# Two heads' values side by side in the array, and a Fourier half of whole 128 by 128 tiles

## The chip, the cores and the metric

The kernel runs on one core of a Trainium2 chip. The metric is the device time of one launch in microseconds (us); lower is better. The core has a matmul engine (TensorE, PE in the profile, with PEld for its weight loads), VectorE (DVE), ScalarE (ACT), GpSimd (POOL) and SyncE (SP), which here issues all DMAs. A matmul holds a stationary operand of up to 128 rows by 128 columns in the array and streams a moving operand of up to 512 columns past it; sums land in PSUM, one PSUM partition for each column of the array.

## The reference

Two layers of an encoder trunk over 512 positions and 1024 channels. Each layer splits its projection into a Fourier group of 512 channels, and 8 query heads, 2 key heads and 2 value heads of 64 channels.

```
h = rmsnorm(x); p = h @ w_in
u, q, k, v = split(p)
y_f = real(fft2(u, norm="ortho")) @ w_fourier + b_fourier
q, k = rope(rmsnorm(q)), rope(rmsnorm(k))
y_a = attention(q, k, v)      # blocks of 128 queries against a band of 384 keys, |i-j| <= 128, a sink logit per head
x = x + concat(rmsnorm(y_f), rmsnorm(y_a)) @ w_o
h = rmsnorm(x)
gate, val = split(dwconv3(h @ w_up))
x = x + (silu(gate) * val) @ w_down
```

## The kernel before

Everything is held transposed or in blocks of 128 positions, so that each matmul has 128 positions or channels on the partitions. In layer 0 the Fourier half and the product of probabilities and values use float32 operands; a float32 matmul shows as two records in the profile. In layer 1 (and in both layers for the large projections) each operand is split in a rounded part and a rest, both float32r, and `mm3` (lines 118 to 122) issues three matmuls of one record each: high by high, rest by high, high by rest. `put` and `split` make such pairs: ScalarE writes the high part, VectorE subtracts it to make the rest.

The Fourier half works on folded data. Since cosines are even and sines odd, 512 columns fold to 257 even ones (0 to 256) and 255 odd ones. They are cut in rows or columns of 128, 128 and 1 for the even part, and 128 and 127 for the odd part. Each of the three steps (the projection `pee`/`poo`, then two transform stages in lines 577 to 606, then the product with `w_fourier` in lines 615 to 643) thus has matmuls with 127 or 1 columns in the array, and the single last row 256 (`tail`, `ut`) meets a one-row table `alts` (tile `altr`) or the last row of W_fourier (`wtr`, `wt`) in matmuls with one row.

Attention goes by pairs of heads (`attention(p, ...)`, p in the order 3, 0, 1, 2). For each head e of the pair and each query block i: scores (line 506), scaling, mask and minimum on VectorE (510), exponential on ScalarE (513), normalising on GpSimd (515), transposition by TensorE (518) and a copy to `pT`. After the four blocks of a head come four matmuls (one for each key block j, line 527) that sum values into `py`. The values lie in `vz`, 64 zero columns on each side and in between, and a window of 128 columns of it is the stationary operand:

```
c0 = 128 * g + 64 * (1 - e)
lhs = [v[:, j, c0:c0 + P] for v in vp]
```

So the head's 64 columns land in the upper or lower half of `py`, and the zeros add nothing to the other half. In layer 1 there are two tiles vz and two pT, high part and rest.

The order on each engine is set by a scheduler that works from the program's dependences and its own cost table; the written order is only its input. It interleaves the Fourier half, attention, and the first half of the output projection (`proj`), whose matmuls are tied to the transpositions in `steps`. PSUM banks are drawn from four pools ("mm" 3, "sc" 2, "tp" 2, "av" 1), and temporary tiles from pools of fixed depth (`TEMPS`). While layer 0's feed-forward part runs, `presplit` loads and splits layer 1's weights and keeps them in DRAM.

Of the kernel before, what the change touches and what calls it, by code (L numbers as in the profile page):

```python
# [16 lines left out]
P = 128  # L17
# [7 lines left out]
NB = S // P  # L25
# [12 lines left out]
def encoder_kernel(tc, t):  # L38
# [34 lines left out]
    TEMPS = {"act": (1024, 8), "m4": (1024, 5), "slab": (1028, 4), "pT": (2560, 2),  # L73
# [75 lines left out]
    def presplit(l):  # L149
# [33 lines left out]
        for j in range(NF):  # L183
            jobs.append((lambda j=j: [wload(t["w_fold"][l, j], 1024, temp(1024, "m4"))], [f"f{j}"]))
# [90 lines left out]
    def zero_values(l):  # L275

        v = [cp.tile([P, NB, 320], F32R if l else F32, tag=f"vz{s}", name=nm("vz")) for s in range(1 + l)]
        for z in v:
            nc.gpsimd.memset(f(z) if l else z, 0.0)
        return v  # L280

    def load_tables(l):
        tab = []
        for i in range(2):
            if l:
                raw = temp(512, "m4")
                nc.sync.dma_start(raw, t["dft"][i])
                tab.append([cp.tile([P, 512], F32R, tag=f"t{z}{i}", name=nm("tab")) for z in "hl"])
                split(*tab[i], raw)
            else:  # L290
                tab.append([cp.tile([P, 512], F32, tag=f"th{i}", name=nm("tab"))])
                nc.sync.dma_start(tab[i][0], t["dft"][i])
        alt = cp.tile([1, 258], F32R if l else F32, tag="altr", name=nm("altr"))
        if l:
            raw = temp(258, "m4")[:1]
            nc.sync.dma_start(raw, t["alt"])
            act(alt, raw)
        else:
            nc.sync.dma_start(alt, t["alt"])
        return tab, alt  # L300

    vp = zero_values(0)
# [33 lines left out]

    def fold_wf(raw, w=None):
        w = temp(512, "tA") if w is None else w
        tt(w[:, :256], raw[:, :256], raw[:, 512:768], ALU.add)
        tt(w[:, 256:], raw[:, 256:512], raw[:, 768:], ALU.subtract)  # L340
        return w
# [11 lines left out]
    for l in range(L):  # L353

        r1 = col_rstd(acc, 1.0 / D)
        qraw = {}
        for grp in (1, 0):
# [16 lines left out]
            for b in range(NB):  # L374
                act(z[:, b, :n], pq[b][:, :n], scale=r1[:, b:b + 1])
                if grp:
                    o = [v[:, b, 64:320].rearrange("p (g d) -> p g d", g=2)[:, :, :64] for v in vp]
                    put(o, pq[b][:, 256:384].rearrange("p (g d) -> p g d", g=2), r1[:, b:b + 1])
# [103 lines left out]
        off = [0, 2, 5, 8]  # L482
# [3 lines left out]
        def attention(p, first_pair):  # L486
            g = p // 2
            py = psum("av")
            first = True
            if not l:  # L490
                both = temp(2560, "pT").rearrange("p (e b q) -> p e b q", e=2, q=P)
            for e in range(2):
                h = 2 * p + e
                nmax, den = [sp.tile([P, NB], F32, tag=z, name=nm(z), bufs=3) for z in ("nmax", "den")]
                if l:
                    pT = temp(2560, "pT", F32R).rearrange("p (s b q) -> p s b q", s=2, q=P)
                    pT = [pT[:, s] for s in range(2)]
                else:
                    pT = [both[:, e]]
                for i in range(NB):  # L500
                    j0, j1 = max(0, i - 1), min(NB - 1, i + 1)
                    n = (j1 - j0 + 1) * P
                    m0 = P if i == 0 else 0
                    sc = psum("sc")
                    for s in range(2):
                        nc.tensor.matmul(sc[:, :n], qT[p][:, e, i * P:(i + 1) * P], kT[g][:, s, j0 * P:(j1 + 1) * P],  # L506
                                         start=s == 0, stop=s == 1)
                    pr = temp(385, "tA")
                    nc.gpsimd.tensor_copy(pr[:, n:n + 1], nsink[:, l, h:h + 1])  # L509
                    nc.vector.tensor_tensor_reduce(  # L510
                        out=pr[:, :n], in0=sc[:, :n], in1=mask[:, m0:m0 + n], scale=qs_scale[p][:, i, e:e + 1],
                        scalar=nsink[:, l, h:h + 1], op0=ALU.add, op1=ALU.min, accum_out=nmax[:, i:i + 1])
                    act(pr[:, :n + 1], pr[:, :n + 1], AF.Exp, scale=-1.0, bias=nmax[:, i:i + 1], accum_out=den[:, i:i + 1])
                    nc.vector.reciprocal(den[:, i:i + 1], den[:, i:i + 1])
                    nc.gpsimd.tensor_scalar(pr[:, :n], pr[:, :n], den[:, i:i + 1], 1.0, op0=ALU.mult, op1=ALU.mult)
                    pp = psum("tp")
                    for j in range(n // P):
                        tr = nc.tensor.transpose(pp[:, j * P:(j + 1) * P], pr[:, j * P:(j + 1) * P], ident)  # L518
                    steps.append(tr.ins)
                    put([z[:, off[i]:off[i] + n // P, :].rearrange("p b q -> p (b q)") for z in pT], pp[:, :n])  # L520
                c0 = 128 * g + 64 * (1 - e)
                for j in range(NB):
                    i0, i1 = max(0, j - 1), min(NB - 1, j + 1)
                    st = off[i0] + j - max(0, i0 - 1)
                    rhs = [z[:, st:st + 2 * (i1 - i0) + 1:2, :] for z in pT]
# [8 lines left out]
        if l == 0:  # L534
            tabs, alts = load_tables(l)
# [23 lines left out]
        def tail_out(pe, scale):  # L559
            b = halves(tp.tile([1, 2, 258], F32R if l else F32, tag="tail", name=nm("tail"), bufs=2))[:1 + l]  # L560
            put(b, pe[2][:1, :258], scale)
            return b

        def stage_out(pe, po, scale):
            tiles = []
            if not l:
                two = temp(1028, "slab")
            for m in range(2):
                a = halves(pair("slab", 514)) if l else [two[:, m * 514:(m + 1) * 514]]
                n = P - m  # L570
                put([z[:, :258] for z in a], pe[m][:, :258], scale)
                put([z[:n, 258:514] for z in a], po[:n, m * 256:(m + 1) * 256], scale)
                tiles.append(a)
            return tiles, tail_out(pe, scale)

        ue, ut = stage_out(pee, poo, 1.0)
        for stage in range(2):
            pe = [psum(), psum(), psum("sc")]
            po = psum()
            for m, (c0, c1) in enumerate(((0, 128), (128, 256), (256, 257))):  # L580
                o = pe[m][:c1 - c0, :258]
                for i in range(2):
                    if stage == 0:
                        mm3(o, [z[:, c0:c1] for z in ue[i]], [z[:, 0:258] for z in tabs[i]], i == 0, False)
                    else:
                        mm3(o, [z[:, c0:c1] for z in tabs[i]], [z[:, 0:258] for z in ue[i]], i == 0, False)
                for z in ut:
                    if stage == 0:
                        nc.tensor.matmul(o, z[:, c0:c1], alts, start=False, stop=z is ut[-1])
                    else:  # L590
                        nc.tensor.matmul(o, alts[:, c0:c1], z, start=False, stop=z is ut[-1])
            for m in range(2):
                n = P - m
                o = po[:n, m * 256:(m + 1) * 256]
                for i in range(2):
                    kn = P - i
                    u2 = [z[:kn, 258:514] for z in ue[i]]
                    t2_ = [z[:kn] for z in tabs[i]]
                    st = m == 0 and i == 0
                    if stage == 0:  # L600
                        mm3(o, [z[:, 1 + m * P:1 + m * P + n] for z in u2], [z[:, 256:512] for z in t2_],
                            st, i == 1, skip_group_check=True)
                    else:
                        mm3(o, [z[:, 257 + m * P:257 + m * P + n] for z in t2_], u2,
                            st, i == 1, skip_group_check=True)
# [9 lines left out]
        for j in range(NF):  # L615
# [3 lines left out]
            wtr = sp.tile([1, P], F32, tag="wtr", name=nm("wtr"), bufs=1)  # L619
            nc.sync.dma_start(wtr, t["w_fourier"][l, 256:257, c0:c1])  # L620
            if l:
# [218 lines left out]
```

## Time and profile before

| | before |
|---|---|
| median of 3 runs | 1075.63 us (1074.64 to 1077.24) |
| the profiled execution | 1076.12 us |
| its span | 1074.3 us |
| TensorE busy / weight loads | 1060.8 us (99%) / 881.9 us (82%) |
| VectorE, ScalarE, GpSimd busy | 737.2, 510.4, 118.4 us |
| DMA | 142.13 MB, 132 GB/s over the span |

All times in the profile count from the span's start. The tiled stages of layer 0 that the change touches lie between about 60 and 158 us, those of layer 1 between about 550 and 680 us; the rest is projections and the feed-forward part. "Busy" of a TensorE record runs to its modelled end, which overlaps the next record's start: how fast matmuls follow one another is read from their starts. In a row of the timeline stand the start, the time to the end of the last record, the engine, the line, the operation, out<-in, the array's rows\*columns in use, the moving operand, and the count.

### The profile page before, as it was taken

The page shows a single profiled execution, that of the slowest core. Times are in us where ns is not written, and L with a number is a line of the kernel's source. Part 1 is how long each engine was busy: PE and PEld are TensorE (multiplying, and loading weights), DVE is VectorE, ACT ScalarE, POOL GpSimd, SP SyncE. Part 2 cuts the span into 40 slices and gives each one's busy share as a digit, 9 for nine tenths or more (in the row PEclk, how much of TensorE's full clock was granted, in tenths as well). Part 3 has the DMA queues.
Part 4 walks back from the last instruction along what each step waited for, and adds up shares of the span by engine and source line. Part 5 has one row for each costly group of instructions (what it writes and reads, how often), then busy time and mean ns, then how long its engine had stood idle before and what let it go on. Part 6 is the DMA issues. An engine that isn't in the chain of part 4 may idle for free.

```text
span 1074.3 us, 14345 instructions
## 1 busy us (share of the span) xinstructions
PE 1060.8 (99%) x5075; PEld 881.9 (82%) x5075; DVE 737.2 (69%) x1364; ACT 510.4 (48%) x940; POOL 118.4 (11%) x171
## 2 busy tenths in 40 slices
PE   8999999999999999999999999999999999999998
PEld 7866888888888888888899887888888888888887
DVE  7856767697767777776619788387887336777632
ACT  5338755454544445455414775155554224444421
POOL 1134410000000000000001442001211000101000
PEclk9999999999999999999999999999999999999999
DMA  7242162333259932338856322423332333233241
GB/s 276 83 138 84 36 196 79 99 98 98 86 174 372 367 99 97 99 104 297 299 182 212 112 70 79 138 79 99 98 99 81 101 106 100 85 102 94 81 147 47
DMA packets 58859, 142.13 MB, mean 132 GB/s; under 512 B 6554, under 2 KB 19108, under 8 KB 58788
## 3 DMA queue, kind: packets, MB, share of 16 engines
q1 hardware_dynamic: 58788, 141.22, 40.3%
q8 instruction: 40, 0.66, 0.3%
q14 instruction: 31, 0.25, 0.1%
HBM read 118.12 MB, written 23.07 MB: 131 GB/s over the span
## 4 chain that ended last, share of the span: by engine, by line
PE 92%; DVE 4%; ACT 1%; DMA 1%; issue 1%; SPq 0%; POOL 0%; DVEq 0%; ACTq 0%
PE ps L120 27%; PE ps L122 27%; PE ps L121 27%; PE ps L118 5%; PE ps L506 2%; PE ps L518 2%; DMA wraw<-in_w_qkv_dram 1%; DVE act L93 1%; PE ps L224 1%; DVE tF L96 1%; PE ps L217 1%; DVE tA L510 0%; PE ps L464 0%; DVE tF L93 0%; DVE slab L93 0%
## 5 line engine op out<-in xcount | busy, mean ns | idle before, releaser
L90 ACT ACTIVATE whi<-wraw 128x512 fp32r<-128x512 f32 (+1 forms) x296 | 181.9, 616 | 297.8 <-PE ps L122 281.4
L93 DVE TENSOR_TENSOR wlo<-wraw,whi 128x512 fp32r<-128x512 f32 (+1 forms) x304 | 221.9, 732 | 115.5 <-ACT whi L90 113.9
L120 PE MATMUL ps<-act,whi 128*128 128x512 f32 x768 | 298.9, 390 | 0.0
L121 PE MATMUL ps<-act,wlo 128*128 128x512 f32 x768 | 298.7, 389 | 0.0
L122 PE MATMUL ps<-act,whi 128*128 128x512 f32 x768 | 298.4, 389 | 0.0
L122 PEld LDWEIGHTS ps<-act,whi 128*128 128x128 f32 x768 | 144.2, 188 | 29.9
L121 PEld LDWEIGHTS ps<-act,wlo 128*128 128x128 f32 x768 | 144.2, 188 | 29.9
L120 PEld LDWEIGHTS ps<-act,whi 128*128 128x128 f32 x768 | 144.2, 188 | 29.8
L96 DVE SCALAR_TENSOR_TENSOR tF<-tF,pb,tF 128x511 f32<-128x511 f32 x176 | 133.2, 763 | 10.6 <-ACT tF L90 8.1
L93 DVE TENSOR_TENSOR tF<-ps,rb 128x512 f32<-128x512 f32 x104 | 71.1, 689 | 76.8 <-PE ps L122 65.2
L120 PE MATMUL ps<-slab,whi 128*128 128x512 f32 (+2 forms) x212 | 83.0, 391 | 1.4 <-ACT slab L90 1.4
L121 PE MATMUL ps<-slab,wlo 128*128 128x512 f32 (+2 forms) x212 | 81.0, 382 | 0.0
L122 PE MATMUL ps<-slab,whi 128*128 128x512 f32 (+2 forms) x212 | 81.0, 384 | 0.0
L90 ACT ACTIVATE tF<-tF,pb 128x512 f32<-128x512 f32 x88 | 71.5, 815 | 8.7 <-DVE tF L93 2.3
L93 POOL TENSOR_TENSOR tF<-tF,tF 128x512 f32<-128x512 f32 x22 | 29.6, 1347 | 257.5 <-DVE tF L96 244.8
L93 DVE TENSOR_TENSOR x<-x,ps 128x512 f32<-128x512 f32 (+1 forms) x49 | 32.9, 673 | 36.3 <-PE ps L122 36.2
L509 POOL COPY tA<-nsink 128x1 f32<-128x1 f32 x64 | 15.0, 243 | 356.8 <-DMA wraw<-in_w_down_dram 321.3
L120 PE MATMUL ps<-pT,whi 128*128 128x512 f32 (+1 forms) x132 | 50.9, 385 | 0.0
L121 PE MATMUL ps<-pT,wlo 128*128 128x512 f32 (+1 forms) x132 | 50.7, 384 | 0.0
L122 PE MATMUL ps<-pT,whi 128*128 128x512 f32 (+1 forms) x132 | 50.6, 383 | 0.0
L120 PEld LDWEIGHTS ps<-slab,whi 128*128 128x128 f32 x212 | 39.8, 188 | 9.4 <-ACT slab L90 1.6
L122 PEld LDWEIGHTS ps<-slab,whi 128*128 128x128 f32 x212 | 39.8, 188 | 8.6 <-DVE nmax L510 0.2
(171 smaller groups left out, 1589.7 us busy)
## 6 DMA issues: line engine op xcount, KB each, us to landing
wraw<-in_w_up_dram SPq DMA_DIRECT2D x88, 512.0 KB, 3.5
wraw<-in_w_down_dram SPq DMA_DIRECT2D x32, 512.0 KB, 3.5
kept<-tA SPq DMA_DIRECT2D x56, 256.0 KB, 5.5
whi<-kept SPq DMA_DIRECT2D x28, 256.0 KB, 2.9
wlo<-kept SPq DMA_DIRECT2D x28, 256.0 KB, 4.2
kept<-tA SPq DMA_DIRECT2D x32, 192.0 KB, 3.3
wraw<-in_w_down_dram SPq DMA_DIRECT2D x32, 192.0 KB, 3.3
wraw<-in_w_o_dram SPq DMA_DIRECT2D x8, 512.0 KB, 3.4
```

The lines of the kernel that those rows point to most:

```text
L90: return nc.scalar.activation(out, in_, func, **kw)
L93: return (eng or nc.vector).tensor_tensor(out, a, b, op=op)
L96: return nc.vector.scalar_tensor_tensor(out=out, in0=a, scalar=s, in1=b, op0=op0, op1=op1)
L118: nc.tensor.matmul(out, a[0], b[0], start=start, stop=stop, **kw)
L120: nc.tensor.matmul(out, a[0], b[0], start=start, stop=False, **kw)
L121: nc.tensor.matmul(out, a[1], b[0], start=False, stop=False, **kw)
L122: nc.tensor.matmul(out, a[0], b[1], start=False, stop=stop, **kw)
L217: nc.tensor.matmul(pt[:, 2 * b:2 * b + 2], acc[:, b * P:(b + 1) * P], ones2, start=True, stop=True)
L224: nc.tensor.matmul(pt[:, b * P:(b + 1) * P], r[:, b:b + 1].to_broadcast([P, P]), ident, start=True, stop=True)
L506: nc.tensor.matmul(sc[:, :n], qT[p][:, e, i * P:(i + 1) * P], kT[g][:, s, j0 * P:(j1 + 1) * P], start=s == 0, stop=s == 1)
L509: nc.gpsimd.tensor_copy(pr[:, n:n + 1], nsink[:, l, h:h + 1])
L518: tr = nc.tensor.transpose(pp[:, j * P:(j + 1) * P], pr[:, j * P:(j + 1) * P], ident)
```

## The change

The Fourier half is cut so that every matmul has 128 rows and 128 columns. Odd columns are moved by one place, so that place 256 holds a zero (or what belongs to the even part's last column) and 257 to 511 the 255 odd ones; the last even column of the projection is computed with 127 odd ones beside it, as a third tile of 128 columns, whose output is written with the wanted column at place 0 and 256 others behind it (`turned`). `alts` and the last row of W_fourier become tiles of 128 rows, zero but for the first row. The tables of `dft` come in five DMAs (two before), the last row of W_fourier in one per layer (four before), and the folded weights of W_fourier as half as many columns, folded by one sum and one difference, with a cleared row.

In attention the two heads of a pair are worked on together, first for query blocks 0 and 1, then for 2 and 3 (`half`). Their values are the 64 columns themselves, with no zeros around; head e writes the 64 partitions of `py` from 64e, so that its stationary operand takes 64 columns of the array, the left or the right ones. There are 6 such matmuls for each half, the heads alternating, with 256 or 128 columns streamed, 12 for a pair and 96 in all (before 32 in layer 0, and 32 times three in layer 1). They are float32 in both layers, and `vp` and `pT` of layer 1 have no rest any more, so that VectorE's subtractions for them go.

```diff
-            for e in range(2):
-                h = 2 * p + e
...
-                for i in range(NB):
+            for half in range(2):
+                for i in (2 * half, 2 * half + 1):
...
-                    put([z[:, off[i]:off[i] + n // P, :].rearrange("p b q -> p (b q)") for z in pT], pp[:, :n])
...
-                    lhs = [v[:, j, c0:c0 + P] for v in vp]
-                    mm3(py[:, i0 * P:(i1 + 1) * P], lhs, rhs, first, e == 1 and j == NB - 1, skip_group_check=True)
-                    first = False
+                    for e in range(2):
...
+                        act(pT[:, half, e, b0:b0 + n // P, :].rearrange("p b q -> p (b q)"), pp[:, :n])
+                for j in ((0, 1, 2), (1, 2, 3))[half]:
+                    i0, i1 = max(2 * half, j - 1), min(2 * half + 1, j + 1)
+                    b0 = (0, 2, 0, 3)[i0] + j - max(0, i0 - 1)
+                    for e in range(2):
+                        nc.tensor.matmul(py[64 * e:64 * e + 64, i0 * P:(i1 + 1) * P], vp[:, j, 64 * g:64 * g + 64],
+                                         pT[:, half, e, b0:b0 + 2 * (i1 - i0) + 1:2, :], start=(half, j) == (0, 0),
+                                         stop=(half, j) == (1, 3), skip_group_check=True)
...
-                for m, (c0, c1) in enumerate(((0, 128), (128, 256), (256, 257))):
-                    mm3(pee[m][:c1 - c0, :258], [z[:, c0:c1] for z in h], we, st, sp_)
-                mm3(poo[:, 0:256], [z[:, 257:385] for z in h], wo, st, sp_, skip_group_check=True)
-                mm3(poo[:127, 256:512], [z[:, 385:512] for z in h], wo, False, sp_, skip_group_check=True)
+                for m in range(3):
+                    mm3(pee[m][:, :258], [z[:, m * P:(m + 1) * P] for z in h], we, st, sp_)
+                for m in range(2):
+                    mm3(poo[:, m * 256:(m + 1) * 256], [z[:, 256 + m * P:384 + m * P] for z in h], wo,
+                        st and m == 0, sp_, skip_group_check=True)
...
+            if turned:
+                put([z[:, 1:257] for z in b], pe[2][:, :256], scale)
+                put([z[:, :1] for z in b], pe[2][:, 256:257], scale)
+            else:
+                put(b, pe[2][:, :258], scale)
...
-                        nc.tensor.matmul(o, alts[:, c0:c1], z, start=False, stop=z is ut[-1])
+                        nc.tensor.matmul(o, alts[:, :P], z, start=False, stop=z is ut[-1])
...
-            mm3(pu[:, :258], wt, ut, False, True)
+            mm3(pu[:, :258], [z[:, c0:c1] for z in wt], ut, False, True)
...
+        nc.vector.memset(w[:1, 256:384], 0.0)
```

How the program's order on TensorE changes, in three places. The second operand after the arrow is the moving one's partner; the size is that of the output, so 1x258 is a matmul with one column in the array. First the first transform stage of layer 0, before (`ps` 695 to 698 are its four banks, `slab` the even and odd parts, `tail` the last row):

```order
L118 MATMUL ps_695<-tab_506,slab_688 128x258
L118 MATMUL ps_697<-tab_506,slab_688 1x258
L118 MATMUL ps_695<-tab_508,slab_688 128x258
L118 MATMUL ps_696<-tab_506,slab_688 128x258
L118 MATMUL ps_696<-tab_508,slab_688 128x258
L118 MATMUL ps_697<-tab_508,slab_688 1x258
L589 MATMUL ps_695<-altr_510,tail_693 128x258
L589 MATMUL ps_696<-altr_510,tail_693 128x258
L589 MATMUL ps_697<-altr_510,tail_693 1x258
L118 MATMUL ps_698<-tab_506,slab_688 128x256
```

and after (there the banks are 703 to 706):

```order
L118 MATMUL ps_703<-tab_505,slab_695 128x258
L118 MATMUL ps_703<-tab_510,slab_695 128x258
L118 MATMUL ps_704<-tab_505,slab_695 128x258
L118 MATMUL ps_704<-tab_510,slab_695 128x258
L605 MATMUL ps_703<-altr_513,tail_700 128x258
L605 MATMUL ps_704<-altr_513,tail_700 128x258
L118 MATMUL ps_705<-tab_505,slab_695 128x258
L118 MATMUL ps_705<-tab_510,slab_695 128x258
L605 MATMUL ps_705<-altr_513,tail_700 128x258
L118 MATMUL ps_706<-tab_505,slab_695 128x256
```

The number of matmuls is the same; the outputs of one partition are gone, and the L605 ones now have 128 rows.

Second, the values of the first pair of heads in layer 0, before (line 118, `vz`; L506 are scores, L518 transpositions of probabilities):

```order
L118 MATMUL ps_795<-pT_796,vz_124 128x256
L506 MATMUL ps_949<-m_96_543,act_756 128x256 x2
L118 MATMUL ps_795<-pT_796,vz_124 128x384
L518 MATMUL ps_868<-ident,tA_862 128x128 x2
L506 MATMUL ps_962<-m_96_543,act_756 128x384 x2
L118 MATMUL ps_1074<-tail_943,wtr_1076 128x258
L506 MATMUL ps_976<-m_96_543,act_756 128x384 x2
L118 MATMUL ps_795<-pT_796,vz_124 128x384
L118 MATMUL ps_795<-pT_796,vz_124 128x256
```

and after (line 536, `v`; L517 scores, L529 transpositions):

```order
L536 MATMUL ps_803<-pT_808,v_180 64x256
L529 MATMUL ps_878<-ident,tA_872 128x128 x3
L517 MATMUL ps_989<-m_97_550,act_764 128x384 x2
L118 MATMUL ps_1111<-slab_950,whi_1114 128x256 x2
L517 MATMUL ps_1003<-m_97_550,act_764 128x384 x2
L536 MATMUL ps_803<-pT_808,v_180 64x256 x3
L536 MATMUL ps_803<-pT_808,v_180 64x128 x2
L529 MATMUL ps_892<-ident,tA_886 128x128 x3
```

Outputs have 64 partitions now; one matmul stands alone between others, five follow one another, the heads in turn.

Third, the values of a pair in layer 1, before (three matmuls of float32r each, lines 120 to 122):

```order
L120 MATMUL ps_6037<-pT_6040,vz_1868 128x256
L121 MATMUL ps_6037<-pT_6040,vz_1869 128x256
L122 MATMUL ps_6037<-pT_6040,vz_1868 128x256
L120 MATMUL ps_6037<-pT_6040,vz_1868 128x384
L121 MATMUL ps_6037<-pT_6040,vz_1869 128x384
L122 MATMUL ps_6037<-pT_6040,vz_1868 128x384
```

and after:

```order
L536 MATMUL ps_6047<-pT_6052,v_5129 64x256
L517 MATMUL ps_6349<-m_1239_5489,act_5838 128x256 x2
L536 MATMUL ps_6047<-pT_6052,v_5129 64x256 x3
L536 MATMUL ps_6047<-pT_6052,v_5129 64x128 x2
L529 MATMUL ps_6136<-ident,tA_6130 128x128 x3
L536 MATMUL ps_6047<-pT_6052,v_5129 64x128
```

Where three matmuls stood for each key block there is one of float32, in two records, for each head and half, and scores and transpositions stand between the pieces. Over the whole program 42 such pieces stand apart from one another, 26 of them of one matmul; the program before leaves the form of 128 rows and 128 columns 49 times, 18 in layer 0 and 31 in layer 1.

More of the change, by code (lines that the diff above doesn't have):

```diff
@@ L355, in encoder_kernel @@
         r1 = col_rstd(acc, 1.0 / D)
+        vp = cp.tile([P, NB, P], F32, tag="v", name=nm("v"))
         qraw = {}
@@ L481, in encoder_kernel @@
         accA = accum()
-        off = [0, 2, 5, 8]
         steps = []
@@ L488, in attention @@
             py = psum("av")
-            first = True
-            if not l:
-                both = temp(2560, "pT").rearrange("p (e b q) -> p e b q", e=2, q=P)
-            for e in range(2):
-                h = 2 * p + e
[L494 to L499, printed above, removed]
-                for i in range(NB):
+            stats = [[sp.tile([P, NB], F32, tag=f"{z}{e}", name=nm(z)) for z in ("nmax", "den")] for e in range(2)]
+            pT = temp(2560, "pT").rearrange("p (z e b q) -> p z e b q", z=2, e=2, q=P)
+            for half in range(2):
+                for i in (2 * half, 2 * half + 1):
                     j0, j1 = max(0, i - 1), min(NB - 1, i + 1)
@@ L503, in attention @@
                     m0 = P if i == 0 else 0
[L504 to L518, printed above, removed]
@@ L519, in attention @@
-                    steps.append(tr.ins)
-                    put([z[:, off[i]:off[i] + n // P, :].rearrange("p b q -> p (b q)") for z in pT], pp[:, :n])
[L521 to L525, printed above, removed]
-                    lhs = [v[:, j, c0:c0 + P] for v in vp]
-                    mm3(py[:, i0 * P:(i1 + 1) * P], lhs, rhs, first, e == 1 and j == NB - 1, skip_group_check=True)
-                    first = False
+                    b0 = (0, 2, 0, 3)[i]
```

140 lines of the change are left out of this document (73 added, 67 removed).

## The prediction

> **What bounds the kernel now.** I read the page's head, busy times and chain first, to find the engine that sets the end; then the windows of the two mixing stages, to see how full that engine is there; then the timeline of TensorE in those stages, start by start.
>
> ```profile
> span 1074.3 us, 14345 instructions
> PE 1060.8 (99%) x5075; PEld 881.9 (82%) x5075; DVE 737.2 (69%) x1364; ACT 510.4 (48%) x940; POOL 118.4 (11%) x171
> PE 92%; DVE 4%; ACT 1%; DMA 1%; issue 1%; SPq 0%; POOL 0%; DVEq 0%; ACTq 0%
> ```
>
> TensorE is busy for 99% and makes up 92% of the chain. So a change to its stream of matmuls is worth about what it does to that stream, and work on the other engines counts only where TensorE waits. The windows that the change touches (60 to 158 in layer 0, 550 to 680 in layer 1, with one narrow stretch of attention):
>
> ```profile
> core 0: us, PE busy (x) PEld busy (x) DVE busy (x) ACT busy (x) POOL busy (x), PEclk, DMA share, GB/s
> 60.00:158.00 98.00, 95.58 (x483) 72.47 (x483) 64.11 (x179) 67.82 (x174) 35.73 (x61) 1.00 0.33 108
> 550.00:610.00 60.00, 59.88 (x406) 56.04 (x406) 40.10 (x97) 26.22 (x57) 14.26 (x4) 1.00 0.58 187
> 610.00:680.00 70.00, 67.20 (x418) 57.69 (x417) 53.14 (x167) 44.68 (x123) 23.10 (x58) 1.00 0.25 76
> 80.00:100.00 20.00, 17.82 (x103) 12.62 (x101) 12.55 (x43) 17.30 (x47) 7.08 (x17) 1.00 0.34 108
> ```
>
> The first row leaves 2.42 us without a matmul, the third 2.80: little waiting, most of it where ScalarE (17.30 of 20 us, last row) or VectorE is nearly full.
>
> **What a change of the tile's form costs.** "128\*1" is a matmul with 128 rows and one column of the array, "1\*128" one with a single row. A busy time here overlaps its neighbours', so only starts are subtracted. Layer 1, operands in fp32r, one record a matmul:
>
> ```profile
> 590.57 0.28 PE L122 MATMUL ps<-wlo,slab 128*128 128x258 f32 x1
> 590.68 0.28 PE L121 MATMUL ps<-whi,slab 128*1 128x258 f32 x1
> 590.80 0.28 PE L122 MATMUL ps<-wlo,slab 128*1 128x258 f32 x1
> 590.92 0.28 PE L121 MATMUL ps<-whi,slab 128*128 128x256 f32 x1
> ...
> 598.53 0.28 PE L122 MATMUL ps<-tab,slab 128*128 128x258 f32 x1
> 598.75 0.39 PE L589 MATMUL ps<-altr,tail 1*128 1x258 f32 x1
> 599.06 0.39 PE L120 MATMUL ps<-tab,slab 128*128 128x258 f32 x1
> 599.29 0.28 PE L121 MATMUL ps<-tab,slab 128*128 128x258 f32 x1
> 599.41 0.28 PE L122 MATMUL ps<-tab,slab 128*128 128x258 f32 x1
> ```
>
> The even step is 0.12 us. A one-column matmul keeps it: here it costs nothing. Around the one-row matmul the steps are 0.22, 0.31 and 0.23, together 0.40 more than three even ones: about 0.09 at each of the two switches, and 0.11 at each first weight load after one, which is no longer done ahead. Layer 0, operands in fp32, two records a matmul:
>
> ```profile
> 65.86 3.15 PE L118 MATMUL ps<-tab,slab 128*128 128x258 f32 x12
> 68.95 1.65 PE L589 MATMUL ps<-altr,tail 1*128 1x258 f32 x6
> 70.53 2.00 PE L118 MATMUL ps<-tab,slab 128*128 128x256 f32 x8
> 72.37 1.04 PE L475 MATMUL ps<-ident,m 128*128 128x128 f32 x8
> 73.24 1.91 PE L118 MATMUL ps<-slab,tab 128*128 128x258 f32 x8
> ...
> 78.85 2.77 PE L118 MATMUL ps<-slab,whi 128*128 128x258 f32 x12
> 81.46 1.04 PE L464 MATMUL ps<-ident,m 128*128 128x128 f32 x8
> ```
>
> The last pair gives the even step: 2.61/12 = 0.2175. The first twelve (with two one-column matmuls of two records among them) take 3.09, which is 0.48 above it: four switches and one full load, 4 x 0.09 + 0.11 = 0.47. So in fp32 the one-column form is charged, in fp32r it is not. A transposition is lighter on its first load:
>
> ```profile
> 600.83 0.66 PE L464 MATMUL ps<-ident,m 128*128 128x128 f32 x4
> 601.42 0.50 PE L589 MATMUL ps<-altr,tail 1*128 1x258 f32 x2
> ```
>
> Four take 0.59; the eight from 72.37 to 73.24, with no switch about them, take 0.87, so four even ones are 0.435, and 0.59 leaves 0.155: one switch and 0.06.
>
> **Part 1, the Fourier half.** One-row and one-column matmuls become full ones over zeros. The rows above show that such a matmul streams its 258 columns as long as a full one, so the stream itself stays, and the switches go. Counted in the program order: layer 0 has 33 switches, 17 first loads of full width and 2 before transpositions: 33 x 0.09 + 17 x 0.11 + 2 x 0.06 = 5.0 us. Layer 1, without the free fp32r ones, has 30, 23 and 3: 5.4 us. Sum **-10.4 us**, on the path, since TensorE has no slack there (59.88 of 60).
>
> **Part 2, the values.** Before, a head's matmul fills all 128 columns with zeros in one half; 1280 columns are streamed per head.
>
> ```profile
> L118 PE MATMUL ps<-pT,vz 128*128 128x384 f32 x32 | 13.0, 488 | 0.0
> L118 PE MATMUL ps<-pT,vz 128*128 128x256 f32 x32 | 9.5, 379 | 0.0
> L120 PE MATMUL ps<-pT,vz 128*128 128x384 f32 x16 | 5.6, 350 | 0.0
> L93 DVE TENSOR_TENSOR pT<-ps,pT 128x384 fp32r<-128x384 f32 x16 | 8.7, 545 | 2.2 <-ACT pT L90 2.2
> L93 DVE TENSOR_TENSOR pT<-ps,pT 128x256 fp32r<-128x256 f32 x16 | 6.6, 413 | 1.3 <-ACT pT L90 1.3
> ```
>
> Per column a step is 0.2175/258 = 0.843 ns in fp32 (two records) and 0.12/258 = 0.465 ns in fp32r (three records). Layer 0: 8 x 1280 x 2 x 0.843 = 17.3 us before, and the same after when heads follow one another. Layer 1: 8 x 1280 x 3 x 0.465 = 14.3 before; it goes to fp32, 17.3 after: **+3.0 us**.
>
> The new matmuls have a form that no row shows, 64 columns wide. The program order has them in 42 separate blocks (19 and 23), so 84 switches: 84 x 0.09 = 7.6; 17 exits to a full load, 1.9, and 25 to transpositions, 1.5; and 42 first loads of half width, between 0 (one column) and 0.11 (full), taken in the middle, 2.3. Sum **+13.3 us**, bounds 0 (the free fp32r one-column rows) and 15.6 us; I take the charged value, because the charged one-column rows are fp32 and so are the new ones.
>
> The Trainium skill, TensorEngine Tiling (Array Packing), section Key Properties, says that a change of the tiling mode, though not of the tile, drains the array. The trace agrees for one row and for fp32 (0.09 us) and contradicts it for the one-column fp32r rows at 0.12; by the rule the term is the 13.3 us above, by the fp32r rows it would be nothing.
>
> Against this stands that the two heads use disjoint columns and disjoint PSUM partitions, so the second may stream beside the first. Of the 96 new matmuls 54 follow the other head's within a block; each could hide one of its two records: 36 of 256 columns and 18 of 128, 36 x 0.216 + 18 x 0.108 = 9.7 us. Bounds: 0 and 9.7. No row has two matmuls side by side. The nearest has a weight load beside a matmul: PEld is busy for 82% under a PE at 99%, and the even step is the stream's length although 0.28 or more is shown as busy, so the array works on more than one instruction wherever nothing is shared. I therefore take the upper side, less half of a half-width load of 0.055 for each of the 54 (1.5 us): **-8.2 us**.
>
> The Trainium skill, TensorE: Matmul & The Clock Gate, Part 3, measured three column tiles at 2.38 times the speed of one; an estimate from it, 0.79 of full overlap, would hide 7.7 us in place of 8.2.
>
> **Part 3, what the other engines lose and gain.** VectorE loses 32 subtractions of pT in layer 1 (8.7 + 6.6 us), in a window where it is busy for 53.14 of 70 us and TensorE misses 2.80. That can give back 0 to 2.8 us; I take **-1.5**, since some of that idle time is the two norms' serial chain. In layer 0 nothing is taken from ScalarE, which limits 80 to 100; 0 there. The second copy of each turned last tile on ScalarE (layer 1: a subtraction too), the memsets on VectorE and the zeroed rows of folded weights lie beside TensorE's stream in windows where these engines have 17 us and more to spare; without that cover each is some 0.4 us. The tables come in five DMAs in place of two, with two tiny ones moved behind a weight load:
>
> ```profile
> 9.83 1.35 SPq L292 DMA_DIRECT2D tab<-in_dft_dram x2
> 11.53 0.30 SPq L299 DMA_DIRECT2D altr<-in_alt_dram x1
> 12.21 0.23 SPq L620 DMA_DIRECT2D wtr<-in_w_fourier_dram x1
> 12.93 10.31 SPq L129 DMA_DIRECT2D wraw<-in_w_qkv_dram x4
> ```
>
> Two issues took 1.35, so five end near 13.2 and the next weight load moves from 12.93 by 0.3; the other three of that row wait for buffers until 23 anyway. Bounds 0 and 0.5 us, taken as 0. The halved load of folded weights is hidden (DMA share 0.33).
>
> **The sum.** -10.4 + 3.0 + 13.3 - 8.2 - 1.5 = -3.8 us. The profiled execution took 1076.12 us (span 1074.3 and 1.8 around it), so 1072.3; it lies 0.5 above the median of 1075.63, which gives **1071.8**, -0.36%. A change below 0.2%, 2.2 us, can't be told from none in this kernel.
>
> **Rivals.** (a) *The two halves don't stream side by side.* For it: no row shows it, and a narrow matmul is no shorter than a full one. Then 8.2 us come back: +4.4, **1080.0**, slower. It decides from the point where less than 4.4 of the 9.7 us is hidden. (b) *The 64-column form switches free*, as one column in fp32r does. Against it: the fp32 rows. -13.3 more: **1058.5**. (c) *A new wait takes the place.* 26 of the 42 blocks hold one matmul, put as early as its first operand allows, and the values now wait for both heads' probabilities from ScalarE, which is at 17.30 of 20 in the attention of layer 0. If the idle 2.18 of that row and the 2.80 of layer 1 double, 5.0 us are lost: +1.2, **1076.8**, the same. Against it: the number of ScalarE instructions in attention stays.
>
> **How the numbers follow.** Forecast 0.56, (a) 0.26, (b) 0.06, (c) 0.12. The forecast's own range is 1067 to 1076: all of 9.7 hidden, free first loads and 2.8 from VectorE at one end, 4 us hidden at the other. Three quarters of it is faster, the rest the same; (a) is mostly slower, (c) half the same and half slower: faster 0.48, same 0.23, slower 0.29. The range leaves out (b) and reaches to (a) with dear first loads: 1066.5 to 1082.
>
> **What would show it.** Starts in the Fourier stages at an even 0.2175 and 0.12 with no "1\*128" or "128\*1" row; layer 0's ps<-tab,slab stage with 26 records in 5.65 us in place of 6.51. In a block of 64-column matmuls, the first record of a head starting under 0.1 us after the last one of the other head shows overlap; 0.216 for 256 columns throughout shows rival (a). Around a block, steps 0.09 and more above the even ones show the switches. Idle VectorE in 610 to 680, with TensorE fuller, shows part 3. Wrong would make it above all heads in single file, or blocks broken by waits.

## The result, and the profile after

| | before | after |
|---|---|---|
| median | 1075.14 us (1074.41 to 1077.24, 4 runs) | 1065.36 us (1064.72 to 1066.05, 4 runs) |
| ratio, 95% interval | | 0.9906 (0.9892 to 0.992) |
| the profiled execution | 1076.12 us | 1065.23 us |
| its span | 1074.3 us | 1063.4 us |

The change saves 9.8 us by the medians, where 3.8 were forecast. The head, the busy times and the chain on the page of the kernel after:

```profile
span 1063.4 us, 14386 instructions
PE 1050.4 (99%) x5107; PEld 876.5 (82%) x5107; DVE 722.4 (68%) x1340; ACT 507.7 (48%) x939; POOL 115.6 (11%) x168
PE 92%; DVE 4%; ACT 1%; POOL 1%; DMA 1%; issue 1%; SPq 0%; DVEq 0%; ACTq 0%; POOLq 0%
```

TensorE still makes up 92% of the chain, and the time in which it has nothing to do went only from 1074.3 - 1060.8 = 13.5 us to 1063.4 - 1050.4 = 13.0. So nearly all of the gain lies inside TensorE's stream. The windows of the two mixing stages; layer 1's is placed 10 us earlier than the one of before, since the kernel gets there earlier:

```profile
core 0: us, PE busy (x) PEld busy (x) DVE busy (x) ACT busy (x) POOL busy (x), PEclk, DMA share, GB/s
60.00:158.00 98.00, 95.67 (x531) 72.70 (x529) 66.89 (x187) 68.72 (x177) 33.70 (x60) 1.00 0.35 111
600.00:670.00 70.00, 68.91 (x430) 52.31 (x429) 40.94 (x134) 44.69 (x126) 23.84 (x59) 1.00 0.23 73
```

In layer 1's attention VectorE fell from 53.14 of 70 us to 40.94, and TensorE's gaps from 2.80 to 1.09. Against this stands one new wait, in the list of TensorE's waits and in the timeline (the bracket at a row's end is the idle time ahead of it and who ended it):

```profile
PE ps L605 <- DVE tail L96: 1.2, 1, 1.2
```

```profile
594.13 0.50 PE L605 MATMUL ps<-altr,tail 128*128 128x258 f32 x2 [1.23 <-DVE tail L96]
```

TensorE waits there for VectorE's second subtraction for the turned last tile. The first transform stage of layer 0 in the timeline after:

```profile
63.66 1.90 PE L118 MATMUL ps<-tab,slab 128*128 128x258 f32 x8
65.39 1.03 PE L605 MATMUL ps<-altr,tail 128*128 128x258 f32 x4
66.27 1.03 PE L118 MATMUL ps<-tab,slab 128*128 128x258 f32 x4
67.14 0.60 PE L605 MATMUL ps<-altr,tail 128*128 128x258 f32 x2
67.57 1.89 PE L118 MATMUL ps<-tab,slab 128*128 128x256 f32 x8
69.30 0.60 PE L490 MATMUL ps<-ident,m 128*128 128x128 f32 x4
```

Every row is 128\*128, and 26 records take 69.30 - 63.66 = 5.64 us, 0.217 each. And the values, one block of twelve records and one of two:

```profile
109.15 1.30 PE L536 MATMUL ps<-pT,v 128*64 128x256 f32 x12
110.38 0.62 PE L517 MATMUL ps<-m,act 128*128 128x384 f32 x2
```

```profile
91.37 0.65 PE L536 MATMUL ps<-pT,v 128*64 128x256 f32 x2
91.94 0.55 PE L529 MATMUL ps<-ident,tA 128*128 128x128 f32 x3
```

The twelve are eight of 256 columns and four of 128. One after another they would stream for 8 x 0.216 + 4 x 0.108 = 2.16 us; the whole block, with the switch out of it, is over in 1.23. The starts of single records show why: they come in pairs 6 to 8 ns apart, 52 such pairs in the whole kernel. The two heads do stream side by side.

Neither of these explains the gain that was not forecast. It lies far from the change. Four consecutive steps in the last down projection, which the change does not touch, before and then after:

```profile
1040.86 0.39 PE L120 MATMUL ps<-slab,whi 128*128 128x512 f32 x1
1041.09 0.39 PE L121 MATMUL ps<-slab,wlo 128*128 128x512 f32 x1
1041.32 0.40 PE L122 MATMUL ps<-slab,whi 128*128 128x512 f32 x1
1041.56 0.39 PE L120 MATMUL ps<-slab,whi 128*128 128x512 f32 x1
```

```profile
1030.30 0.39 PE L120 MATMUL ps<-slab,whi 128*128 128x512 f32 x1
1030.53 0.39 PE L121 MATMUL ps<-slab,wlo 128*128 128x512 f32 x1
1030.76 0.39 PE L122 MATMUL ps<-slab,whi 128*128 128x512 f32 x1
1030.98 0.39 PE L120 MATMUL ps<-slab,whi 128*128 128x512 f32 x1
```

Three steps take 0.70 us before and 0.68 after. Over 40 us of this projection TensorE, which never idles there, starts 174 matmuls before and 178 after, at the same granted clock and the same DMA share (columns: window, its length, PE busy and count, clock, DMA share, GB/s):

```profile
1020.00:1060.00 40.00, 40.00 (x174) 1.00 0.37 117
```

```profile
1009.00:1049.00 40.00, 40.00 (x178) 1.00 0.37 117
```

The groups by form show the same by operand. Before, the mean busy time of one is 404 ns with `slab` streaming, 395 with `m` and 390 with `act`:

```profile
L120 PE MATMUL ps<-slab,whi 128*128 128x512 f32 x188 | 75.9, 404 | 1.4 <-ACT slab L90 1.4
L120 PE MATMUL ps<-m,whi 128*128 128x512 f32 x93 | 36.7, 395 | 0.0
L120 PE MATMUL ps<-act,whi 128*128 128x512 f32 x768 | 298.9, 390 | 0.0
```

After, the first two are shorter (`act` has the same row as before):

```profile
L120 PE MATMUL ps<-slab,whi 128*128 128x512 f32 x188 | 74.7, 398 | 0.0
L120 PE MATMUL ps<-m,whi 128*128 128x512 f32 x93 | 36.2, 389 | 0.0
```

What connects them to the change is one line of it that the prediction does not name: with 512 in place of 514 columns in the folded parts, the temporary tile `slab` became 1024 floats wide.

```diff
-    TEMPS = {... "slab": (1028, 4), ...
+    TEMPS = {... "slab": (1024, 4), ...
```

A tile of 1028 floats is 4112 bytes per partition and is placed every 4128. In the built program the four slab tiles then begin at 192, 224, 0 and 32 modulo 256 bytes and the m4 tiles behind them (called `m` in the profile) at 64, while the weights `whi` and `wlo`, and `act` and `pT`, begin at 192. With 4096 bytes all of them begin at 192. Mean steps between starts, matmuls of 512 columns in both layers, worked out from all single starts, without the few steps that hold a wait or another matmul:

| streamed tile | before: place, step | after: place, step |
|---|---|---|
| slab, four tiles | 192, 224, 0, 32: 231.8, 232.7, 232.8, 234.0 ns | 192: 227.5 to 227.7 ns |
| m4, five tiles | 64: 232.0 to 233.9 ns | 192: 226.6 to 226.7 ns |
| pT, first and second | 192: 230.4, 227.2 ns | 192: 226.7 ns |
| act, eight tiles | 192: 226.8 to 226.9 ns | 192: 226.8 ns |

With some 520 such steps from slab, 277 from m4 and 372 from pT this sums to about 520 x 5.2 + 277 x 5.9 + 372 x 2.1 ns = 5.1 us.

### The profile page after: what moved, and what is told of

Read it like the earlier page. It is cut to its first block, busy times and chain, and to the rows that moved or that the text cites. A ratio compares the mean times of both kernels' runs of the same rounds, so it can differ in the third digit from the quotient of the medians.

```text
span 1063.4 us, 14386 instructions
## 1 busy us (share of the span) xinstructions
PE 1050.4 (99%) x5107; PEld 876.5 (82%) x5107; DVE 722.4 (68%) x1340; ACT 507.7 (48%) x939; POOL 115.6 (11%) x168
## 4 chain that ended last, share of the span: by engine, by line
PE 92%; DVE 4%; ACT 1%; POOL 1%; DMA 1%; issue 1%; SPq 0%; DVEq 0%; ACTq 0%; POOLq 0%
PE ps L120 27%; PE ps L121 27%; PE ps L122 27%; PE ps L118 3%; PE ps L536 3%; PE ps L529 2%; PE ps L517 2%; POOL qk3r L210 1%; PE ps L224 1%; DVE act L93 1%; PE ps L217 1%; DVE tF L96 1%; DVE tF L93 0%; DVE slab L93 0%; ACT tA L90 0%
## 5 line engine op out<-in xcount | busy, mean ns | idle before, releaser
L93 DVE TENSOR_TENSOR wlo<-wraw,whi 128x512 fp32r<-128x512 f32 (+1 forms) x304 | 219.4, 724 | 100.5 <-ACT whi L90 99.1
L120 PE MATMUL ps<-slab,whi 128*128 128x512 f32 (+2 forms) x212 | 81.7, 386 | 0.0
L122 PE MATMUL ps<-slab,whi 128*128 128x512 f32 (+2 forms) x212 | 80.0, 382 | 0.0
L521 DVE CUSTOM_DVE_ANT_0 tA<-ps,pb,nsink 128x256 f32<-128x256 f32 (+1 forms) x64 | 38.3, 605 | 20.1 <-PE ps L517 15.4
L122 PEld LDWEIGHTS ps<-slab,whi 128*128 128x128 f32 x212 | 39.6, 188 | 8.4 <-issue 1.2
```

Of the source, the lines that this page charges most:

```text
L93: return (eng or nc.vector).tensor_tensor(out, a, b, op=op)
L120: nc.tensor.matmul(out, a[0], b[0], start=start, stop=False, **kw)
L122: nc.tensor.matmul(out, a[0], b[1], start=False, stop=stop, **kw)
L521: nc.vector.tensor_tensor_reduce(out=pr[:, :n], in0=sc[:, :n], in1=mask[:, m0:m0 + n], scale=qs_scale[p][:, i, e:e + 1], scalar=nsink[:, l ...
```

## The experiments

### Is it the width of the slab?

The theory (A): the change does in its own stages about what was forecast, and the rest is the place of the slab tiles. The rival (B): the width means nothing, and the terms of the Fourier half or of the values were mis-sized by as much. The first kernel is the kernel after with the old width, and nothing else changed:

```diff
-    "slab": (1024, 4)
+    "slab": (1028, 4)
```

> The changed kernel with the slab tiles 1028 floats wide again (4 floats unused); every engine's order is the same. Theory A: the part of the gain that the prediction missed comes from where tiles lie: 1028 floats put slab tiles 2 and 4 and all m4 tiles at other offsets, and matmuls that stream from them step 231 to 234 ns in place of 227. Then 512-column matmuls from slab and m4 step 230 ns or more again and the time is about 1071 us (5 to 5.5 us over the changed kernel). Theory B: the missed part is fewer waits and the scheduler's new order; then this kernel takes 1065.4 us, as the changed one, with steps of 227.

Measured: 1070.77 us, ratio 0.9958 (0.9942 to 0.9975); the kernel before, timed beside it, took 1075.87. The window of the down projection and the groups go back to what they were before the change:

```profile
1014.00:1054.00 40.00, 40.00 (x174) 1.00 0.38 117
```

```profile
L120 PE MATMUL ps<-slab,whi 128*128 128x512 f32 x188 | 75.7, 403 | 0.0
L120 PE MATMUL ps<-m,whi 128*128 128x512 f32 x93 | 36.7, 395 | 0.0
```

So the width alone is worth 1070.77 - 1065.36 = 5.4 us, and the change without it 5.1 us (2.7 to 6.2 by the interval).

The next two are the kernel before with the values of two heads side by side (attention and `vp` of the kernel after) and its own Fourier half; they differ from one another in the width of slab alone. 1088 floats are 4352 bytes, 17 times 256, so that all slab tiles begin at the same place modulo 256 though not modulo 4096.

```diff
+        vp = cp.tile([P, NB, P], F32, tag="v", name=nm("v"))
...
+                        nc.tensor.matmul(py[64 * e:64 * e + 64, i0 * P:(i1 + 1) * P], vp[:, j, 64 * g:64 * g + 64],
```

```diff
-    "slab": (1028, 4)
+    "slab": (1088, 4)
```

> The kernel before with the values side by side alone (Fourier half as before, slab 1028). By steps from the traces: 87 more switches of the tile's form, half-width matmuls overlapping as seen, layer 1's values in float32: 7.8 us more of TensorE's stream than before; VectorE's relief gives back 1 to 3. Both theories: 1079 to 1082 us, slower than before. If the values were the gain, it would be under 1073.

> The same with slab tiles of 1088 floats (4352 bytes), so that all slab and m4 tiles lie at the same offset modulo 256 bytes as the act tiles; the order is the same. Theory A: 5 to 5.5 us under the run with 1028, about 1075 us, and steps of 227 from slab and m4. Theory B: the same time as with 1028, within 1 us.

Measured: 1078.89 us, ratio 1.0029 (1.0018 to 1.004), with 1028, and 1073.42 us, ratio 0.9983 (0.9969 to 0.9998), with 1088. Again 5.5 us for the width alone, this time with a larger tile in place of a smaller one. So it is not the size of the tile. The values by themselves make the kernel slower by 3.0 us; 1078.89 lies just under the 1079 to 1082 that was expected.

The fourth is the Fourier part alone: the kernel after with the zero-padded values, head after head, of the kernel before (one buffer in place of two for `rb`, a tile of broadcast scales, for room).

```diff
-        rb = cp.tile([P, 512], F32, tag="rb", name=nm("rb"), bufs=2)
+        rb = cp.tile([P, 512], F32, tag="rb", name=nm("rb"), bufs=1)
...
+    vp = zero_values(0)
...
+                    mm3(py[:, i0 * P:(i1 + 1) * P], lhs, rhs, first, e == 1 and j == NB - 1, skip_group_check=True)
```

> The Fourier part alone: whole tiles in the Fourier half, slab 1024, values as before with zeros around them (and one rb tile in place of two, to make room). No switch of the tile's form is left, 10.5 us less of TensorE's stream than before. Theory A: another 5.5 us from the tiles' place: about 1059 us, faster than the changed kernel by some 6, because the values' 42 blocks cost more than their overlap gives. Theory B: about 1065 us or more.

Measured: 1064.39 us, ratio 0.9893 (0.9878 to 0.9908). It falls between the two theories, nearer to what the rival expects, though the width was just shown to count: the terms -10.4 and -5.4 should give -15.8, and -11.5 came. The window of layer 1's attention:

```profile
600.00:670.00 70.00, 66.77 (x430) 60.10 (x429) 53.59 (x167) 46.29 (x126) 24.17 (x59) 0.98 0.22 73
```

VectorE is as full as before the change, and TensorE's gaps are 3.23 us, 0.4 more than before. The granted clock of 0.98 comes from one stretch of 3.4 us at half the clock, right behind two waits of TensorE, and takes another 1.7 us:

```profile
635.30:638.70 3.40, 3.40 (x13) 0.50 0.02 7
```

With 1.6 us of wait for the turned last tile, 0.4 + 1.7 + 1.6 = 3.7 of the missing 4.3 us are found. So part of the Fourier gain was given back to waits for VectorE, it seemed; the last group takes that up.

### What is the overlap worth, and what places are slow?

The values head by head within each half, so that a head's matmuls follow one another. If the overlap is real (A), most of it is lost; if it is nothing (B), the fewer blocks gain:

```diff
-                for j in ((0, 1, 2), (1, 2, 3))[half]:
+                for e in range(2):
...
-                    for e in range(2):
+                    for j in ((0, 1, 2), (1, 2, 3))[half]:
```

> The changed kernel with the values' matmuls written head by head in each half, not in turn. The program has 34 blocks (42 before) and 14 places (54) where the other head's matmul follows. Theory A (two heads overlap only where one follows the other): 8 blocks fewer save 2.5 us, 40 lost overlaps cost about 8: some 5.5 us slower than the changed kernel, about 1071. Theory B (the gain is not from overlap of the two heads): faster by the 2.5 us, about 1063.

Measured: 1066.58 us, ratio 0.9919 (0.9902 to 0.9936). It lies between the two. The timeline shows the lost overlap, here six records of a single head:

```profile
91.52 1.29 PE L536 MATMUL ps<-pT,v 128*64 128x256 f32 x6
92.74 0.55 PE L529 MATMUL ps<-ident,tA 128*128 128x128 f32 x3
```

These six take 1.22 us, as long as the twelve of both heads above. From the first start of a block to the next matmul's, the 34 blocks of this kernel sum to 34.6 us, the 42 of the kernel after to 30.3; with 0.093 us for the switch into each, 37.8 against 34.2. So 3.6 us are lost, but the whole is slower by only 1.2: the rest came back elsewhere in a changed order; where is open. As to the overlap the trace decides, as to the sum neither theory does.

The opposite: the six matmuls of a half are kept together. The one that needs the last operand goes first, and the others may only be issued behind it:

```diff
+                lead = None
-                for j in ((0, 1, 2), (1, 2, 3))[half]:
+                for j in ((0, 1, 2), (2, 3, 1))[half]:
...
-                    for e in range(2):
-                        nc.tensor.matmul(...
+                    for e in (1, 0):
+                        with tc.issue_after(lead) if lead is not None else nullcontext():
+                            mm = nc.tensor.matmul(...
+                        lead = lead or mm.ins
```

> The changed kernel with the six matmuls of values of each half kept together: the first of them needs the probabilities that come last, and the others are issued after it. 16 blocks in place of 42, 80 places with the other head following in place of 54. By the traces' steps the stream is 12.4 us shorter (26 excursions of 0.31, and 4.6 us more overlap). Theory A (TensorE's stream is the bound): 1053 to 1058 us. Theory B (values issued later make new waits that eat it): 1063 us or more.

Measured: **1052.12 us** (1051.6 to 1053.83), ratio 0.979 (0.9775 to 0.9804), the best of all, below both kernels and 1 us under what was expected at best. Head of its page, and one of its 16 blocks:

```profile
span 1050.1 us, 14391 instructions
PE 1035.2 (99%) x5107; PEld 873.3 (83%) x5107; DVE 721.2 (69%) x1340; ACT 506.9 (48%) x939; POOL 117.5 (11%) x168
```

```profile
92.48 1.30 PE L538 MATMUL ps<-pT,v 128*64 128x256 f32 x12
93.71 0.55 PE L529 MATMUL ps<-ident,tA 128*128 128x128 f32 x3
```

All blocks look like this: 16 in 19.7 us, plus 16 x 0.093 for the switches in, 21.2 against 34.2 in the kernel after, 13.0 us less. All 96 pairs of records start together, 52 in the kernel after. That the spans differ by about as much, 13.3, is in part luck: the profiled execution of the kernel after spent a stretch at half the clock that this one did not (first the kernel after, then this one):

```profile
27.30:30.70 3.40, 3.40 (x14) 0.50 0.00 1
27.30:30.70 3.40, 3.40 (x23) 1.00 0.01 5
```

This is worth about 1.7 us, which leaves 11.6 for the change; and TensorE's idle time grew from 13.0 to 1050.1 - 1035.2 = 14.9 us, with the waits for `tA` and `pT` in the list of its waits going from 0.8 to 3.0. So theory B has a small part too: values that are issued later do make new waits, of some 2 us.

Then the place. Everything that is streamed (the temporary tiles) is moved by 128 bytes against the weights, with no other change to the work:

```diff
+    padt = tp.tile([P, 32], F32, tag="padt", name="padt", bufs=1)
+    nc.gpsimd.memset(padt, 0.0)
     zero = temp(512, "sq")
```

> The changed kernel with 128 bytes put ahead of the pool of temporary tiles: act, pT, slab and m4 tiles all move by 128 bytes, the weights whi and wlo stay. TensorE's order is the same. Theory A1 (a step is 227 ns where the streamed tile lies at the same offset modulo 256 bytes as the weights, or at this very offset, and 231 to 234 elsewhere): now all 512-column matmuls step 231 or more, also those from act, some 15 to 20 us more: 1080 to 1085. Theory A2 (what costs is tiles at offsets that differ among themselves): 1065 us, steps of 227.

Measured: 1084.43 us, ratio 1.0091 (1.0075 to 1.0108), the slowest of all, 19 us above the kernel after. Now `act`, whose steps were right in every kernel so far, is slow too:

```profile
L120 PE MATMUL ps<-act,whi 128*128 128x512 f32 x768 | 303.0, 395 | 0.0
```

All its tiles begin at 64 modulo 256, and the mean steps are 231.7 to 232.9 ns, whatever tile is streamed.

One more width, with a single run: 1056 floats, 4224 bytes, so that slab tiles begin at 192 and 64 in turn and all others at 192.

```diff
-    "slab": (1024, 4)
+    "slab": (1056, 4)
```

> The changed kernel with slab tiles of 1056 floats (4224 bytes): tiles 1 and 3 keep the offset of the act tiles modulo 256 bytes, 2 and 4 lie 128 off, the m4 tiles keep it. Theory A1: matmuls from slab 2 and 4 step 231 to 234 ns, those from the others and from m4 227: 1066.5 to 1068 us. Theory A3 (tiles must lie at the same offset modulo 4096 bytes): m4 too is slow, 1069 to 1071.

Measured: 1068.88 us in one run (span 1067.1), between the ranges of the two theories. The m4 tiles stay fast (226.7 to 227.5 ns), against A3, but A1 fails on slab: the slab tiles at 64 step by 230.8 ns, those at 192 by 231.9: also slow, though they lie where they should. In the projections a slab tile is streamed right after another, and the `pT` tile that follows slab is slow as well (231.1 ns), the second one not (227.3). So a tile in the right place right behind a misplaced one is slow too. It wears off: in the kernel before, the six steps of the first `pT` tile behind slab are 232.9, 232.3, 229.9, 231.5, 228.7 and 226.7 ns, and a slab tile is streamed for three steps only. Why, no run here shows.

### Is it the place as such, and was it VectorE?

Weights and temporary tiles are moved together by 128 bytes. If the place in memory counts, this is as slow as the shift above; if the place relative to the weights counts, nothing changes.

```diff
+    padt = cp.tile([P, 32], F32, tag="padt", name="padt")
+    nc.gpsimd.memset(padt, 0.0)
```

> The changed kernel with 128 bytes put ahead of the weights' pool, so that weights whi and wlo and all temporary tiles move together by 128 bytes; TensorE's order is the same. Theory A1r (what counts is where the streamed tile lies against the weights): steps of 227, 1065 us. Theory A1p (what counts is the place itself, modulo 256 bytes): steps of 232, 1084 us, as when the temporary tiles alone were moved.

Measured: 1065.42 us, ratio 0.991 (0.9893 to 0.9926); the kernel after has 1065.36. It is the place relative to the weights.

Last, the Fourier part alone once more, with layer 1's values and probabilities in float32, still zero-padded and head after head. This takes VectorE's subtractions away and makes the values' stream 3.0 us longer by the forecast's steps. It also lets the two heads of a pair share one `pT` tile, where in layer 1 each head took one of the two.

```diff
-        v = [cp.tile([P, NB, 320], F32R if l else F32, tag=f"vz{s}", name=nm("vz")) for s in range(1 + l)]
+        v = [cp.tile([P, NB, 320], F32, tag="vz0", name=nm("vz"))]
...
+                pT = [both[:, e]]
```

> The kernel with the Fourier part alone, but layer 1's values and probabilities in float32, one tile each, with zeros around the values as in layer 0: VectorE's subtractions for them are gone, TensorE's stream is 3.4 us longer (17.3 us of values for 14.0), no switch of form. Theory A (in f_only the gain was lost again to waits for VectorE in layer 1's attention, 6 us more than in the changed kernel, and taking its subtractions away gives them back): 1060 to 1063 us, and TensorE's idle time between 600 and 670 falls from 3.2 us to about 1. Theory B (those waits come from the order of work, not from VectorE's load): 1067 to 1069.

Measured: 1062.01 us, ratio 0.9879 (0.9865 to 0.9894): with a stream 3.0 us longer it is not slower than the Fourier part alone, but 2.4 us faster by the medians and 1.5 by the ratios (whose intervals overlap). The window:

```profile
600.00:670.00 70.00, 69.30 (x408) 59.28 (x409) 41.78 (x134) 44.14 (x126) 24.25 (x59) 1.00 0.27 77
```

VectorE went from 53.59 to 41.78 us, TensorE's gaps from 3.23 to 0.70, the clock back to 1.00. So beside a shortened Fourier half VectorE's load limits this stretch, and taking it away is worth 4.5 to 5.4 us (1.5 or 2.4, and the 3.0 of the longer stream). In the profiles 2.5 of this are gaps and 1.7 the stretch at half the clock; whether that stretch came of the waits, and what the shared `pT` tile gives, is not shown.

## Why the prediction was right or wrong

The direction was right, and the time fell below the range, because the sum lacked a term. The step that failed is "The sum": it adds up parts 1 to 3, which look at the two mixing stages and at the loads ahead of them, and so puts the matmuls of the projections and the feed-forward part at no change, without a reason. These stream from the tile `slab` and from the m4 tiles behind it, and the change made slab 1024 floats wide in place of 1028, which no part mentions. The runs showed that this width is worth 5.4 us by one pair of kernels and 5.5 by another. With the old width the change takes 1070.77 us, against a forecast of 1071.8, and inside its own range of 1067 to 1076. The profile of before held the clue in the groups by form: the same 128x512 matmul at 404, 395 and 390 ns, by the tile that is streamed.

Point by point, for the change at the old width (-5.1 us measured, -3.8 forecast):

- **The Fourier switches** (-10.4). The size was right where it can be read: layer 0's transform stage takes 5.64 us, as forecast 5.65, with no one-row or one-column matmul left. The kernel with the Fourier part alone and float32 values fits the sum: -10.4, +3.0 of stream, -5.4 of place, 0.70 - 2.80 = -2.1 of gaps and +1.2 of the new wait are -13.7, and 1062.01 - 1074.97 = -13.0 was measured.
- **The values' own stream** (+3.0) and **the switches around their blocks** (+13.3). In the 42 blocks a switch in takes 0.093 us and one out 0.094, a first load of 64 columns 0.05 (0.267 between the first two records in place of 0.216), a transposition's first load behind it 0.055. With the full loads at 0.11 as in the trace of before, that is 42 x 0.237 + 25 x 0.055 + 17 x 0.11 = 13.2 us. The fp32 rows were the right choice, and rival (b), free switches, falls.
- **The overlap** (-8.2, bounds 0 and 9.7). It is larger than its upper bound: from the blocks' 30.3 us go 42 x (0.05 + 0.094) = 6.0 for the first loads and the switches out, and the 24.3 left are 10.2 less than the 34.5 of single file. The bound assumed that a matmul can hide one of its two records; in a block of twelve both are hidden. Rival (a), single file, falls. The Trainium skill, TensorEngine Tiling (Array Packing), section Key Properties, says that different tiles load and multiply in parallel; the trace agrees, with starts 6 to 8 ns apart and twelve records in the time of six.
- **VectorE's relief** (-1.5). TensorE's gaps in layer 1's attention fell by 2.80 - 1.09 = 1.7 us.
- **The second copy of the turned tile** ("beside TensorE's stream"). Wrong in layer 1: TensorE waits 1.23 us for it. The cover named, spare time of VectorE over the window, says nothing about a chain of two subtractions in which the second is needed at once. This is rival (c) in another place, at its size.

With these in place of the forecast's terms the sum is -10.4 + 3.0 + 13.2 - 10.2 - 1.7 + 1.2 = -4.9 us, against -5.1 measured without the new width. That the forecast's -3.8 lies so near is in part luck: an overlap 2.0 us larger paid for a wait of 1.2 that was put at nothing, and the interval of the measured -5.1 (2.7 to 6.2) is too wide to tell -3.8 from -4.9. By itself neither half shows its own term so cleanly: the values alone gave +3.0 us, where these terms give 3.0 + 13.2 - 10.2 - 1.7 = +4.3, at the edge of the interval (+1.9 to +4.3).

## What to carry to other kernels

Where a change alters the size of a tile in a shared pool, look at everything that streams from that pool and at every tile placed behind it: here a width of 1028 in place of 1024 floats cost 5.4 us in stages that the change did not touch, and rows of one form with different means per operand show it. Narrow matmuls pay when they come in blocks with both halves of the array at work: twelve records in one block cost a switch in and out once, and the same 96 matmuls took 34.2 us in 42 blocks and 21.2 in 16. In 16 blocks, with the whole Fourier tiles, the kernel takes 1052.12 us, against 1062.01 with zero-padded float32 values. When a scheduler cuts such a block up, tie it together.

## What the runs showed of the hardware that was not expected

- A step of a 512-column float32r matmul takes 227 ns when the streamed tile begins at the same place modulo 256 bytes as the weights, and 231 to 234 ns when it begins 32, 64, 96 or 128 bytes off (128 also where all tiles are off alike; 32, 64 and 96 only among tiles of other places). Moving all streamed tiles by 128 bytes costs 19 us; moving the weights with them costs nothing. That 256 counts follows from the tiles 4352 bytes apart, which are as good as those 4096 apart, and from the shift by 128, which is bad; offsets that are no multiple of 32 were not tried.
- A tile in the right place that is streamed behind misplaced ones is slow as well (slab at 192: 231.9 ns; the first `pT`: 231.1, the second 227.3), until after some steps it is fast again. What carries over is open.
- Two tiles of 64 columns run at twice the speed of one: 6 records of one head and 12 of both both take 1.22 to 1.23 us.
